# Pass 1 of a hybrid decoder layer: the work behind each turning transfer issued after k's and q's; triangles turned in pass 1, q and k kept by 512 tokens

## The chip, the cores and the metric

One core of a Trainium2 chip runs the whole program. The metric is the device time of one execution in microseconds (us), the median of three runs. A smaller time is better.

## What is computed

One decoder layer over 2048 tokens of width 1024, all in float32 to the outside. In the reference, cut to what matters:

```python
a = _rmsnorm(h, g_in[i])                                   # 2048 x 1024
z = einsum('bsd,de->bse', a, w_in[i])                      # 1024 -> 4*512 + 3*512
q, k, v, gate_b, u_a, v_a, gate_a = split(z)
q = _rope(_rmsnorm(q, q_norm[i]), positions)               # 8 heads of 64
k = _rope(_rmsnorm(k, k_norm[i]), positions)
o_b = _dilated_attention(q, k, v) * silu(gate_b)           # (window, dilation): (128,1),(512,4),(2048,16)
o_a = _gmlp_spatial(u_a, v_a, w_spatial[i], b_spatial[i], ln_v_g[i], ln_v_b[i]) * silu(gate_a)
h = h + einsum('bse,ed->bsd', concatenate([o_b, o_a]), w_out[i])
gate = sigmoid(_rmsnorm(h, g_ple[i]) @ w_ple_gate[i] + b_ple_gate[i])
h = h + gate * (p[i] @ w_ple_proj[i])
```

`_gmlp_spatial` multiplies each chunk of 128 tokens by four lower triangles of 128x128 (`w_spatial`), which must be turned (transposed) once. The three branches of the attention are merged with weights from their softmax denominators.

## The kernel before, in words

**Pass 1** (0 to 388 us) goes over 16 tiles of 128 tokens. `prep(n)` makes the normed and turned tile: sum of squares on ACT (L210), scale on DVE (L147, L216) with a power on POOL (L148), a copy of the 16-bit halves of each word to two staging tiles on ACT (L179), two transposing DMAs on SP's queue (L181), a copy back on DVE (L183), and a split of each half into a high part on ACT (L193) and a low part on DVE (L194). The result is the tile `aT`. It then stores the turned tile (L499) and loads the x of a later tile (L233). `turn_p` does the same with the tile p of the per-layer input, without the split.

`step(n, g)` multiplies `aT` of tile n with the weights of one of q, k, v and the gate g of the attention, 24 matmuls of 128x512 each (L227), in the PSUM banks `mm`, `s`, `av` and `gt`. After k's and q's product `post_qk` squares on ACT (L405), reduces on DVE (L407), rotates with two products on DVE (L413, L415) and a sum on POOL (L114), takes a power on POOL (L148), scales on DVE (L420), and splits the result into a high half `hl` on ACT (L422) and a low half on DVE (L423). `turn_qk` turns `hl` with one transposing DMA into `st` (L429); for k an ACT copy regroups `st` (L432); then it is stored to d_q or d_k (L435). `post_v` scales and stores v (L442, L443), `post_gb` takes a tanh on ACT (L451) and a multiply on DVE (L452), which free the gate's bank.

Within pass 1 a scheduler sets the order of every engine's instructions from the data they need and its own estimate of when each is ready. The code's order is only its start. Every engine works through its list in that order: an instruction that waits holds up what stands behind it on the same engine. `issue_after(i)` allows nothing that is issued inside it to be placed before instruction i. PE's order is written by hand from the last two tiles of pass 1 on.

**Pass 2** (388 to about 860 us) is the attention, four pairs of heads with 38 steps each (scores L755, exponentials, turning of the weights by DMA L777, values L791). Into it PE's order mixes the three gMLP products u, v_A and gate_A as filler (L627): first `BLOCK0` us of them ahead of the first scores, then `FILL` us per step. Their weights come in 24 pieces of 256 KB through four staging tiles called `raw` (L127, copied by L133 on ACT and DVE and L135 on POOL). q and k come from d_q and d_k in chunks (`load_qk`), the chunks of the next pair during the steps of the current one. **Pass 3** (860 to 1293 us) is the output projection and the per-layer embedding.

Buffers that matter here: `stage()` hands out the `raw` tiles in turn; `aT` has two buffers in one pool and one in another; the x of tile n+2 is loaded into the buffer that tile n leaves.

Of the kernel before, what the change touches and what calls it, by code (L numbers as in the profile page):

```python
# [10 lines left out]
F32 = mybir.dt.float32  # L11
# [43 lines left out]
BLOCK0, FILL = 18, 1.3  # L55
# [9 lines left out]
STAGE = {"g": "m1 m2 vt hl st", "q": "m1 m2 vt hl st", "k": "vt", "v": ""}  # L65
# [16 lines left out]
def hybrid_layer(ctx: ExitStack, tc: tile.TileContext, io, out):  # L82
# [11 lines left out]
    d_qk = [dram.tile([128, HEADS, S], F16, name=f"d_{n}") for n in "qk"]  # L94
# [10 lines left out]
    cst.tile([128, 16], F32, name="pad")  # L105
# [66 lines left out]
    def turn_words(src, turned):  # L172
# [24 lines left out]
    def turn_rows(src, dst, turned):  # L197
        turn_words(src, turned)
        split_words(turned, dst)
# [6 lines left out]
    def norm_T(xt, xn, pool, turned=None, gain=None):  # L206
# [10 lines left out]
        if turned is None:  # L217
            split_T(xn, 8, aT, whole=gain is not None)
        else:
            turn_rows(xn, aT, turned)  # L220
# [48 lines left out]
    with ExitStack() as s1, ExitStack() as s1q:  # L269
# [6 lines left out]
        ORDER = "gqkv"  # L276
# [114 lines left out]
        TAB = {}  # L391
# [10 lines left out]
        def post_qk(n, which, ps):  # L402
# [19 lines left out]
            nc.scalar.activation(hl[:, :, 0], r, AF.Copy)  # L422
            nc.vector.tensor_tensor(hl[:, :, 1], r, hl[:, :, 0], op=OP.subtract)  # L423
            return hl

        def turn_qk(n, which, hl):
# [8 lines left out]
            nc.sync.dma_start(d_qk[which][:, :, n * 128:(n + 1) * 128], st)  # L435
# [13 lines left out]
        def post_gb(n, ps):  # L449
            g = p1g.tile([128, 512], F32, name="gb")  # L450
# [6 lines left out]
        def gm_constants():  # L457
            for name, src in (("lng", bcast(io["ln_v_g"], 512)), ("lnb", bcast(io["ln_v_b"], 512)),
                              ("mask", io["c_mask"]), ("bs", io["b_spatial"][0].rearrange("g t -> t g")),
                              ("gg", io["w_spatial"][0].rearrange("g t s -> t g s"))):  # L460
                shape = {"mask": [128, 512], "bs": [128, 4]}.get(name, [128, 512])
                CG[name] = pg.tile(shape, F32, name=name)
                dst = CG[name]
                nc.sync.dma_start(dst if name != "gg" else dst.rearrange("p (g s) -> p g s", g=4), src)

        def spatial_weights():

            wsT, gg, bs = pg.tile([128, 4, 128], F32, name="wsT"), CG["gg"], CG["bs"]
            CG["wsT"] = wsT
            keep = stage()[:, 0:128]  # L470
            nc.vector.tensor_scalar(keep, CG["mask"][:, 384:512], 0.0, None, op0=OP.is_ge)
            pt = bank("pt", (128, 4, 128))
            for g in range(4):
                w = gg[:, g * 128:(g + 1) * 128]
                last = nc.vector.scalar_tensor_tensor(w, w, 0.25, keep, op0=OP.mult, op1=OP.mult)
                nc.tensor.transpose(pt[:, g], w, ident)
            nc.vector.tensor_copy(wsT, pt)
            with tc.issue_after(last.ins):
                nc.vector.tensor_scalar(bs, bs, 0.25, None, op0=OP.mult)
# [11 lines left out]
        def prep(n):  # L491
            if n < NT:
                xt = XT.pop(n)
# [463 lines left out]
```

## Time and profile before

| | |
|---|---|
| Median of three runs | 1290.81 us (1289.02, 1290.81, 1296.98) |
| Profiled execution | 1295.01 us, span 1293.2 us |
| PE busy | 1201.3 us, 93% of the span |
| DVE, ACT, POOL busy | 888.2 (69%), 648.9 (50%), 512.1 us (40%) |
| Mean granted clock of TensorE | 0.976 |
| PE by stage | 0 to 40 us start; 160 to 340 us 168.41 of 180 busy; 388 to 442 us 33.24 of 54 busy; 860 to 1293 us 420.87 of 433 busy |

A granted clock of 1.00 is TensorE at 2.4 GHz, 0.50 at 1.2 GHz. PE is the engine to watch: on it each gap has an engine or a DMA that ended last, and the profile names it in brackets behind the row.

### The profile page before, as it was taken

The numbers are of one execution on the slowest core, as the hardware profiler recorded it, in microseconds if no ns is written. First come the engines' busy times: TensorE is split into PE (matmuls) and PEld (weight loads), VectorE is DVE, ScalarE is ACT, GpSimd is POOL, SyncE is SP. The second block draws the span as 40 slices with busy tenths as digits, with TensorE's granted clock in tenths as the row PEclk, the third lists the DMA queues.
The fourth block names the chain that finished last, engine by engine and source line by source line (L and its number), as shares of the span: only waits on it lengthen the run. The fifth ranks groups of instructions, "written<-read, shape, count | busy, mean of one in ns | idle before, by whom it ended". The sixth has DMA issues, their size and how long they took to land.

```text
span 1293.2 us, 21329 instructions
## 1 busy us (share of the span) xinstructions
PE 1201.3 (93%) x7166; PEld 976.0 (75%) x7166; DVE 888.2 (69%) x2253; ACT 648.9 (50%) x1273; POOL 512.1 (40%) x454
## 2 busy tenths in 40 slices
PE   5999999989995799899799799879999999999998
PEld 4778877767884687687687688768778888888887
DVE  5885565655575678778778678598766766666733
ACT  5754334334344577677677677444334434434422
POOL 4852343433453456555555565342212121221100
PEclk9999999999997899899999999989999999999999
DMA  7598777776769899999999999955555655654531
GB/s 263 160 229 197 168 183 166 165 180 157 175 171 239 202 202 220 219 216 236 218 217 223 219 229 215 207 176 174 141 147 123 165 156 128 153 162 127 143 90 49
DMA packets 442254, 233.21 MB, mean 180 GB/s; under 512 B 337440, under 2 KB 392864, under 8 KB 442144
## 3 DMA queue, kind: packets, MB, share of 16 engines
q1 hardware_dynamic: 442144, 231.85, 75.4%
q8 instruction: 56, 0.92, 0.3%
q14 instruction: 54, 0.44, 0.1%
HBM read 102.66 MB, written 57.28 MB: 124 GB/s over the span
## 4 chain that ended last, share of the span: by engine, by line
PE 41%; DMA 19%; DVE 16%; ACT 7%; issue 7%; POOL 6%; SPq 4%; DVEq 0%; ACTq 0%; POOLq 0%
PE mm L227 17%; PE mm L627 8%; PE gt L227 5%; DMA pt<-raw 4%; DMA xt<-raw 3%; PE s L227 3%; DMA st<-hl 3%; PE s L755 3%; PE pt L791 2%; DVE aT L194 2%; DMA ob<-d_o 2%; ACT raw L179 2%; POOL rsh L148 2%; DVE m L420 1%; DVE pr L758 1%
## 5 line engine op out<-in xcount | busy, mean ns | idle before, releaser
L227 PE MATMUL mm<-wslot,aT 128*128 128x512 f32 x1536 | 362.8, 392 | 7.8 <-ACT aT L193 3.3
L227 PEld LDWEIGHTS mm<-wslot,aT 128*128 128x128 f32 x1536 | 289.4, 189 | 70.4 <-ACT aT L193 4.6
L627 PE MATMUL mm<-wslot,aT 128*128 128x512 f32 x1152 | 317.9, 418 | 23.2 <-DVE raw L618 14.2
L627 PEld LDWEIGHTS mm<-wslot,aT 128*128 128x128 f32 x1152 | 214.1, 197 | 63.5 <-DVE raw L618 14.6
L114 POOL TENSOR_TENSOR raw<-pr,raw 128x512 f16<-128x512 f32 (+1 forms) x152 | 178.0, 1177 | 151.6 <-ACT raw L773 137.9
L766 ACT ACTIVATE pr<-pr,ost 128x256 f32<-128x256 f32 (+1 forms) x384 | 150.5, 451 | 78.8 <-DVE ost L764 70.9
L227 PE MATMUL gt<-wslot,aT 128*128 128x512 f32 x744 | 177.8, 393 | 6.1 <-DVE gb L452 5.3
L227 PEld LDWEIGHTS gt<-wslot,aT 128*128 128x128 f32 x744 | 139.8, 189 | 38.0 <-DVE gb L452 7.0
L791 PEld LDWEIGHTS <-pt 128*128 128x128 f16 x1800 | 66.3, 99 | 62.1 <-issue 33.7
L773 ACT ACTIVATE raw<-pr 128x512 f16<-128x512 f32 (+1 forms) x152 | 93.2, 620 | 39.6 <-DMA pt<-raw 37.4
L791 PE MATMUL pt<-sv,pt 128*128 128x65 f16 x1800 | 83.6, 196 | 21.8 <-DMA pt<-raw 21.8
L758 DVE CUSTOM_DVE_ANT_0 pr<-s,mask 128x256 f32<-128x256 f32 (+1 forms) x256 | 81.3, 359 | 29.7 <-POOL raw L114 16.0
L227 PE MATMUL av<-wslot,aT 128*128 128x512 f32 x360 | 86.0, 392 | 7.3 <-DVE gb L452 6.3
L227 PE MATMUL s<-wslot,aT 128*128 128x512 f32 x384 | 90.0, 390 | 1.6 <-POOL wslot L135 1.6
L114 POOL TENSOR_TENSOR m<-m,m 128x512 f32<-128x512 f32 x32 | 47.9, 1498 | 94.8 <-DVE rsh L147 88.8
L227 PEld LDWEIGHTS av<-wslot,aT 128*128 128x128 f32 x360 | 67.2, 188 | 23.6 <-DVE gb L452 7.9
L227 PEld LDWEIGHTS s<-wslot,aT 128*128 128x128 f32 x384 | 72.0, 188 | 17.0 <-POOL wslot L135 2.0
L755 PEld LDWEIGHTS <-sq 128*128 128x128 f16 x768 | 70.4, 121 | 13.7 <-issue 7.4
L755 PE MATMUL s<-sk,sq 128*128 128x256 f16 (+1 forms) x512 | 73.7, 279 | 7.0 <-DMA sk<-d_k 6.1
L566 POOL TENSOR_TENSOR ma<-ob,ma 128x512 f32<-128x512 f32 x16 | 24.5, 1533 | 122.1 <-DMA ma<-d_gb 58.0
L563 POOL TENSOR_TENSOR ob<-ob 128x512 f32<-128x512 f32 x16 | 21.0, 1314 | 126.5 <-DVE ob L561 126.5
L764 DVE TENSOR_SCALAR ost<-ost 128x2 f32<-128x2 f32 (+1 forms) x152 | 66.9, 442 | 2.6
(209 smaller groups left out, 1723.4 us busy)
## 6 DMA issues: line engine op xcount, KB each, us to landing
xt<-x SPq DMA_DIRECT2D x32, 512.0 KB, 4.6
d_o<-ost SPq DMA_DIRECT2D x48, 264.0 KB, 3.2
raw<-w_in SPq DMA_DIRECT2D x38, 256.0 KB, 3.7
sv<-d_vt SPq DMA_DIRECT2D x32, 264.0 KB, 3.5
ob<-d_o SPq DMA_DIRECT2D x16, 528.0 KB, 4.6
xt<-d_at SPq DMA_DIRECT2D x16, 512.0 KB, 5.0
out<-th SPq DMA_DIRECT2D x32, 256.0 KB, 2.8
d_at<-raw SPq DMA_DIRECT2D x28, 256.0 KB, 2.5
```

Of the source, the lines that this page charges most:

```text
L114: nc.gpsimd.tensor_tensor(dst, a, b, op=op)
L148: nc.gpsimd.tensor_tensor(dst, dst, mhalf[:, :width], op=OP.pow)
L179: nc.scalar.activation(turned[t].bitcast(U16), words[:, t], AF.Copy)
L194: nc.vector.tensor_tensor(lo, f, hi.bitcast(F32), op=OP.subtract)
L227: nc.tensor.matmul(ps, aT[:, ha, k, :], w(slot, hw, k), start=(n == 0), stop=(n == 3 * nk - 1))
L627: nc.tensor.matmul(ps, GT[c][:, ha, k, :], slots[g][:, hw, k, :], start=(n == 0), stop=(n == 23))
L755: nc.tensor.matmul(ps[:, c:c + nk], cols(br, j, Q[h]), cols(br, j, K, n, h, self.nb), start=(n == 0), stop=(n == 1))
L758: nc.vector.tensor_tensor_reduce(pr[:, c:c + nk], ps[:, c:c + nk], mask[:, m - nk:m], -1.0, 3e38, op0=OP.add, op1=OP.min, accum_out=o[:, j ...
L764: nc.vector.tensor_scalar(nm, nm, math.log(PSCALE), None, op0=OP.add)
L766: nc.scalar.activation(pr[:, c:c + nk], pr[:, c:c + nk], AF.Exp, bias=o[:, j - j0, 130 + h:131 + h], scale=-1.0)
L773: nc.scalar.activation(ph, pr[:, :width], AF.Copy)
L791: nc.tensor.matmul(PO[0][:, j % 2, h], self.pt[:, t, c // 128], vt[:, h, vv, 0:65], start=(n == 0), stop=(n == 3 * self.nb - 1))
```

## The change

It has five parts. (1) In pass 1 k's product comes ahead of q's, and what follows a turning transfer of x or p (copy back, split, stores, load of the next x) is collected in `rest` and issued by `finish` behind the last two instructions of q's `post_qk` of the tile before. (2) The triangles are turned at tile 3 of pass 1 and kept in DRAM (`d_ws`) until pass 2 loads them. (3) d_q and d_k are laid out by 512 tokens; a chunk is two loads of q (128 KB) and two of k (256 KB), where it was two of q and four of k; the last two chunks of a pair come apart and not as one. A narrow step (256 wide) is turned by one DMA, where it was two. (4) The gates of the last two tiles go to `raw` tiles; the first gMLP chunk uses its pool's tile and not a `raw` tile. (5) `BLOCK0` goes from 18 to 11.

```diff
-BLOCK0, FILL = 18, 1.3
+BLOCK0, FILL = 11, 1.3
...
-STAGE = {"g": "m1 m2 vt hl st", "q": "m1 m2 vt hl st", "k": "vt", "v": ""}
+STAGE = {"g": "m1 m2 vt hl st", "k": "m1 m2 vt hl st", "q": "vt", "v": ""}
...
-    d_qk = [dram.tile([128, HEADS, S], F16, name=f"d_{n}") for n in "qk"]
...
+    d_qk = [dram.tile([128, 4, HEADS, 512], F16, name=f"d_{n}") for n in "qk"]
+    d_ws = dram.tile([128, 512], F32, name="d_ws")
...
-        for i in range(2):
-            nc.vector.tensor_copy(turned[i].bitcast(U16).rearrange("p (k c t) -> p t k c", t=2, k=nk),
-                                  halves[:, :, i * nk:i * nk + nk])
+        def back():
+            for i in range(2):
+                nc.vector.tensor_copy(turned[i].bitcast(U16).rearrange("p (k c t) -> p t k c", t=2, k=nk),
+                                      halves[:, :, i * nk:i * nk + nk])
+        if rest is None:
+            back()
+        else:
+            rest.append(back)
...
-    def turn_rows(src, dst, turned):
-        turn_words(src, turned)
-        split_words(turned, dst)
+    def turn_rows(src, dst, turned, rest=None):
+        turn_words(src, turned, rest)
+        if rest is None:
+            split_words(turned, dst)
+        else:
+            rest.append(lambda: split_words(turned, dst))
...
-    def norm_T(xt, xn, pool, turned=None, gain=None):
+    def norm_T(xt, xn, pool, turned=None, gain=None, rest=None):
...
     AT, GT, XT, slots = {}, {}, {0: xt0}, {}
     usc = cst.tile([128, 1], F32, name="usc")
-    def load_qk(qk, hp, c, n=1):
-        tl = slice(512 * c, 512 * (c + n))
+    def load_qk(qk, hp, c):
+        hs = slice(2 * hp, 2 * hp + 2)
         for h in range(2):
-            nc.sync.dma_start(qk[0][h][:, tl], d_qk[0][:, 2 * hp + h, tl])
-            yield
+            nc.sync.dma_start(qk[0][h][:, 512 * c:512 * c + 512], d_qk[0][:, c, 2 * hp + h])
+        yield
+        src = d_qk[1][0:64, c, hs]
         for i in (0, 64):
-            for t in range(2):
-                nc.sync.dma_start(qk[1][i:i + 64, t, :, tl], d_qk[1][64 * t:64 * t + 64, 2 * hp:2 * hp + 2, tl])
-            yield
+            nc.sync.dma_start(qk[1][i:i + 64, c].rearrange("p t h s -> p t (h s)"),
+                              bass.AP(tensor=src.tensor, offset=src.offset,
+                                      ap=[[4 * HEADS * 512, 64], [64 * 4 * HEADS * 512, 2], [1, 1024]]))
+        yield
     gating, s2 = ExitStack(), ExitStack()
     with ExitStack() as s1, ExitStack() as s1q:
...
-        ORDER = "gqkv"
+        ORDER = "gkqv"
...
             r = m1.rearrange("p h t d -> p h (t d)")
             nc.vector.tensor_tensor(r, r, rs[:, :, None].to_broadcast([128, HEADS, 64]), op=OP.mult)
             hl = p1.tile([128, HEADS, 2, 64], F16, name="hl", bufs=2)
-            nc.scalar.activation(hl[:, :, 0], r, AF.Copy)
-            nc.vector.tensor_tensor(hl[:, :, 1], r, hl[:, :, 0], op=OP.subtract)
+            LAST[:] = [nc.scalar.activation(hl[:, :, 0], r, AF.Copy).ins,
+                       nc.vector.tensor_tensor(hl[:, :, 1], r, hl[:, :, 0], op=OP.subtract).ins]
             return hl
         def turn_qk(n, which, hl):
...
-            nc.sync.dma_start(d_qk[which][:, :, n * 128:(n + 1) * 128], st)
+            nc.sync.dma_start(d_qk[which][:, n // 4, :, n % 4 * 128:n % 4 * 128 + 128], st)
...
-            g = p1g.tile([128, 512], F32, name="gb")
+            g = p1g.tile([128, 512], F32, name="gb") if n < NT - 2 else stage()
...
 def spatial_weights():
+            gg, keep = stage(), stage()
+            nc.sync.dma_start(gg.rearrange("p (g s) -> p g s", g=4),
+                              io["w_spatial"][0].rearrange("g t s -> t g s"))
+            nc.sync.dma_start(keep[:, 0:128], io["c_mask"][:, 384:512])
+            nc.sync.dma_start(bs, io["b_spatial"][0].rearrange("g t -> t g"))
+            nc.vector.tensor_scalar(keep[:, 0:128], keep[:, 0:128], 0.0, None, op0=OP.is_ge)
+            ps = bank("pt", (128, 4, 128))
+                nc.vector.scalar_tensor_tensor(w, w, 0.25, keep[:, 0:128], op0=OP.mult, op1=OP.mult)
+                nc.tensor.transpose(ps[:, g], w, ident)
+            nc.vector.tensor_copy(gg, ps.rearrange("p g s -> p (g s)"))
+            nc.sync.dma_start(d_ws, gg)
+            nc.vector.tensor_scalar(bs, bs, 0.25, None, op0=OP.mult)
...
             else:
                 (post_v if g == "v" else post_gb)(n, ps)
-        def prep(n):
-            if n < NT:
-                xt = XT.pop(n)
-                turned = None if n < PE1 else (stage(), stage())
-                AT[n] = norm_T(xt, xt, p1g if n % 3 == 2 else stream, turned, gbc)
+        def prep(n, rest=None):
+            xt = XT.pop(n)
+            turned = None if n < PE1 else (stage(), stage())
+            AT[n] = norm_T(xt, xt, p1g if n % 3 == 2 else stream, turned, gbc, rest)
+            def store():
                 if turned is None:
                     nc.sync.dma_start(d_at[n], xt)
                 for i, t in enumerate(turned or ()):
                     nc.sync.dma_start(d_at[n][:, 512 * i:512 * i + 512], t)
-                tables(n)
                 if n + 2 < NT:
                     XT[n + 2] = load_x(x_t[n + 2])
-        def turn_p(n):
+            tables(n)
+            if rest is None:
+                store()
+            else:
+                rest.append(store)
+        def turn_p(n, rest):
             t = stage()
             pp, turned = two(t)
             nc.sync.dma_start(pp, io["p"][0, 0][n * 128:(n + 1) * 128])
-            turn_words(pp, two(turned))
-            nc.sync.dma_start(d_p[n], turned)
+            turn_words(pp, two(turned), rest)
+            rest.append(lambda: nc.sync.dma_start(d_p[n], turned))
+        def finish(rest):
+            with tc.issue_after(LAST[0]), tc.issue_after(LAST[1]):
+                for f in rest:
+                    f()
         prep(0)
         prep(1)
...
                 v_scale()
             for n in range(2):
                 step(n, g)
-        for n in range(2, NT - 2):
-            prep(n)
-            for m in range(max(0, n - 4) * NT // 10, max(0, n - 3) * NT // 10):
-                turn_p(m)
-            if n > 2:
-                for g in "qkvg":
+        for n in range(2, NT):
+            rest = []
+            prep(n, rest)
+            if n == 3:
+                spatial_weights()
+            for m in range(max(0, n - 4) * NT // 10, min(NT, max(0, n - 3) * NT // 10)):
+                turn_p(m, rest)
+            if n == 2:
+                for f in rest:
+                    f()
+                continue
+            if n < NT - 1:
+                for g in "kq":
                     step(n - 1, g)
-        for g in "qkvg":
-            step(NT - 3, g)
-        prep(NT - 2)
-        prep(NT - 1)
+            finish(rest)
+            if n < NT - 1:
+                for g in "vg":
+                    step(n - 1, g)
         in_order = ExitStack()
         in_order.enter_context(tc.manual_schedule(engines={mybir.EngineType.PE}))
         XT[0] = load_x(d_at[0])
         gm_rows(0, stream)
-        for g in "qkv":
+        for g in "kqv":
             for n in (NT - 2, NT - 1):
                 step(n, g)
         s1q.close()
...
-            t = pool.tile([128, 512], F32, name=name, bufs=n) if c else stage()
+            t = pool.tile([128, 512], F32, name=name, bufs=n)
...
-                self.pt = pt = p2.tile([128, 2, 4, 128], F16, name="pt", bufs=PH)
-                if width == 512:
-                    nc.sync.dma_start_transpose(pt.rearrange("p t k q -> p (t k) q"),
-                                                hl.rearrange("p t c -> p (t c)"))
-                else:
-                    for t in range(2):
-                        nc.sync.dma_start_transpose(pt[:, t, :width // 128], hl[:, t, :width])
+                pt = p2.tile([128, 8, 128], F16, name="pt", bufs=PH)[:, 0:width // 64]
+                nc.sync.dma_start_transpose(pt, hl.rearrange("p t c -> p (t c)"))
+                self.pt = pt.rearrange("p (t k) q -> p t k q", t=2)
...
-                        h, c = {10: (1, 0), 11: (1, 1), 0: (0, 2)}.get(i % 12, (4, 0))
-                        loads = load_qk(qk, hp + h, c, 1 + c // 2) if i > 1 and hp + h < 4 else iter(())
+                        h, c = {10: (1, 0), 11: (1, 1), 0: (0, 2), 1: (0, 3)}.get(i % 12, (4, 0))
+                        loads = load_qk(qk, hp + h, c) if i > 1 and hp + h < 4 else iter(())
```

Names: `LAST` is filled by `post_qk`; `two(t)` gives the halves of a staging tile; `rows_T` gives an `aT`; the lines of the changed kernel are some 10 to 33 higher than before.

**ACT, one tile in the middle of pass 1.** Before (`gb` is the gate's tanh, `aT,ss<-xt` the sum of squares, `hl<-st` the regrouping of the turned k, `raw<-xt` the copy of x's words, `raw<-raw` that of p's, `sq` the squares of q's or k's product, `hl<-m` the high half; `mm` holds q's product and `s` k's):

```order
L451 ACTIVATE gb<-gt 128x512
L210 ACTIVATE aT,ss<-xt 128x1024
L432 ACTIVATE hl<-st 128x1024
L179 ACTIVATE raw<-xt 128x1024 x2
L405 ACTIVATE sq<-mm 128x512
L179 ACTIVATE raw<-raw 128x256 x2
L193 ACTIVATE aT<-raw 128x512
L405 ACTIVATE sq<-s 128x512
L193 ACTIVATE aT<-raw 128x512
L422 ACTIVATE hl<-m_2118 128x8x64
L442 ACTIVATE vt<-gt,sv 128x8x64
L422 ACTIVATE hl<-m_2163 128x8x64
```

and in the changed kernel, from k's high half of one tile to q's squares of the next:

```order
L436 ACTIVATE hl<-m_1155 128x8x64
L456 ACTIVATE vt<-av,sv 128x8x64
L446 ACTIVATE hl<-st 128x1024
L436 ACTIVATE hl<-m_1201 128x8x64
L465 ACTIVATE gb<-gt 128x512
L202 ACTIVATE aT<-raw 128x512 x2
L183 ACTIVATE raw<-xt 128x1024 x2
L222 ACTIVATE aT,ss<-xt 128x1024
L183 ACTIVATE raw<-xt 128x1024
L419 ACTIVATE sq<-s 128x512
L183 ACTIVATE raw<-raw 128x256 x2
L419 ACTIVATE sq<-mm 128x512
```

The two splits to `aT` stood among the squares of q's and k's; they now stand behind q's high half and the gate's tanh, ahead of k's squares of the tile that they are for. k's regrouping moved ahead of q's high half.

On PE the 96 matmuls of a tile came as 24 of q, 24 of k, then v and the gate. Now come 4 of k, 4 of q and 4 of the gate, then the rest of k and of q, so that k's last is the 33rd and q's last the 52nd, then 24 of v and the other 20 of the gate.

**DVE, the same place in the changed kernel** (`L188` copies back, first x's and then p's; `L203` is the low part of `aT`, `L466` frees the gate's bank):

```order
L434 TENSOR_TENSOR m_961<-m_961,rsh 128x512
L437 TENSOR_TENSOR hl<-m_961,hl 128x8x64
L457 SCALAR_TENSOR_TENSOR vt<-gt,sv,vt 128x8x64
L434 TENSOR_TENSOR m_1007<-m_1007,rsh 128x512
L437 TENSOR_TENSOR hl<-m_1007,hl 128x8x64
L188 COPY raw<-xt 128x2x512 x2
L188 COPY raw<-raw 128x2x128 x2
L466 SCALAR_TENSOR_TENSOR gb<-gb,av 128x512
L203 TENSOR_TENSOR aT<-raw,aT 128x512 x2
L150 TENSOR_SCALAR rs<-ss 128x1
```

The copies back stand behind q's low half (`hl<-m_1007,hl`); before, they stood between the rotation of q and that of k.

**SP's queue at the end of pass 1.** Before (`w_in` is the weights' pieces, `st<-hl` the turning of q or k):

```order
L127 DMA raw<-w_in 128x512 x4
L429 DMA_TRANSPOSE st<-hl 128x8x128
L127 DMA raw<-w_in 128x512 x2
L435 DMA d_q<-st 1024x1x128
L127 DMA raw<-w_in 128x512 x2
L429 DMA_TRANSPOSE st<-hl 128x8x128
L127 DMA raw<-w_in 128x512
L435 DMA d_q<-st 1024x1x128
L127 DMA raw<-w_in 128x512 x2
```

and in the changed kernel:

```order
L475 DMA mask<-c_mask 128x512
L475 DMA wsT<-d_ws 128x512
L475 DMA lng<-ln_v_g 128x512
L475 DMA lnb<-ln_v_b 128x512
L467 DMA d_gb<-raw 128x512
L273 DMA sq_3472<-d_q 128x512
L130 DMA raw<-w_in 128x512 x2
L467 DMA d_gb<-raw 128x512
L130 DMA raw<-w_in 128x512
L273 DMA sq_3473<-d_q 128x512
```

The pieces stood among q's and k's last transfers; all 24 now stand behind the last stores of pass 1 and the first load of q, whose tile `sq` takes room that pass 1 held until its last matmul.

**SP's queue towards the second pair of heads.** Before:

```order
L265 DMA sk<-d_k 64x2x512 x2
L777 DMA_TRANSPOSE pt<-raw 128x8x128
L672 DMA d_oa<-gg 128x512
L265 DMA sk<-d_k 64x2x512 x2
L777 DMA_TRANSPOSE pt<-raw 128x8x128
L261 DMA sq_3454<-d_q 128x1024
L729 DMA sv<-d_vp 128x4x264
L777 DMA_TRANSPOSE pt<-raw 128x8x128
L261 DMA sq_3455<-d_q 128x1024
L781 DMA_TRANSPOSE pt<-raw 128x2x128 x2
L800 DMA d_o<-ost 128x528
L265 DMA sk<-d_k 64x2x1024 x2
```

and in the changed kernel:

```order
L277 DMA sk<-d_k 64x2x1024
L809 DMA_TRANSPOSE pt<-raw 128x8x128
L277 DMA sk<-d_k 64x2x1024
L273 DMA sq_3472<-d_q 128x512
L809 DMA_TRANSPOSE pt<-raw 128x8x128 x2
L762 DMA sv<-d_vp 128x4x264
L829 DMA d_o<-ost 128x528
L809 DMA_TRANSPOSE pt<-raw 128x8x128
L809 DMA_TRANSPOSE pt<-raw 128x4x128
L809 DMA_TRANSPOSE pt<-raw 128x8x128 x2
L273 DMA sq_3473<-d_q 128x512
L277 DMA sk<-d_k 64x2x1024 x2
```

Four loads of k for a chunk became two of twice the width, and the narrow turning (`L781`, two of 128x2x128) became one (128x4x128).

## Rows read from the trace of the kernel before

**Rows 1.** PE by stretch: us, busy (instructions), granted clock, DMA share, GB/s.

```profile
160.00:340.00 180.00, 168.41 (x733) 1.00 0.72 170
340.00:388.00 48.00, 48.00 (x213) 1.00 0.73 177
...
860.00:1293.00 433.00, 420.87 (x1848) 0.99 0.50 136
```

**Rows 2.** PE's timeline in pass 1: start, us, operation [idle before <-releaser].

```profile
268.57 5.60 PE L227 MATMUL gt<-wslot,aT 128*128 128x512 f32 x24
274.01 5.60 PE L227 MATMUL mm<-wslot,aT 128*128 128x512 f32 x24
...
287.29 5.74 PE L227 MATMUL gt<-wslot,aT 128*128 128x512 f32 x24 [2.24 <-DVE gb L452]
```

**Rows 3.** DVE's timeline in pass 1.

```profile
269.60 0.69 DVE L407 TENSOR_REDUCE ssh<-sq 128x8 f32<-128x512 f32 x1 [3.82 <-ACT sq L405]
...
270.80 0.74 DVE L415 TENSOR_TENSOR m<-mm,tb 128x256 f32<-128x256 f32 x2
271.46 0.16 DVE L147 TENSOR_SCALAR rsh<-ssh 128x8 f32<-128x8 f32 x1
...
273.90 1.40 DVE L183 COPY raw<-xt 128x1024 uint16<-128x1024 uint16 x2 [2.28 <-DMA xt<-raw]
...
277.62 0.68 DVE L420 TENSOR_TENSOR m<-m,rsh 128x512 f32<-128x512 f32 x1
...
279.48 1.27 DVE L147 TENSOR_SCALAR rsh<-ssh 128x8 f32<-128x8 f32 x1
...
284.56 0.68 DVE L420 TENSOR_TENSOR m<-m,rsh 128x512 f32<-128x512 f32 x1
285.94 0.69 DVE L423 TENSOR_TENSOR hl<-m,hl 128x512 f16<-128x512 f32 x1 [0.69 <-ACT hl L422]
```

**Rows 4.** ACT's timeline in pass 1.

```profile
268.99 0.58 ACT L405 ACTIVATE sq<-mm 128x512 f32<-128x512 f32 x1
...
274.75 0.64 ACT L193 ACTIVATE aT<-raw 128x512 fp32r<-128x512 f32 x1 [2.40 <-DVE raw L183]
...
285.82 0.58 ACT L451 ACTIVATE gb<-gt 128x512 f32<-128x512 f32 x1
...
290.63 1.11 ACT L432 ACTIVATE hl<-st 128x1024 f16<-128x1024 f16 x1 [3.20 <-DMA st<-hl]
```

**Rows 5.** POOL's timeline in pass 1.

```profile
277.78 0.84 POOL L396 TENSOR_TENSOR ta<-gA,cs 128x128 f32<-128x128 f32 x1 [3.09 <-DVE m L413]
279.11 1.60 POOL L114 TENSOR_TENSOR m<-m,m 128x512 f32<-128x512 f32 x1 [0.49 <-DVE m L415]
```

**Rows 6.** PE's timeline in pass 2, a longer wait.

```profile
504.05 0.54 PE L791 MATMUL pt<-sv,pt 128*128 128x65 f16 x12 [2.40 <-DMA pt<-raw]
...
504.79 2.75 PE L627 MATMUL mm<-wslot,aT 128*128 128x512 f32 x6
```

**Rows 7.** PE by stretch, behind that wait (columns as in rows 1).

```profile
506.00:508.00 2.00, 2.00 (x16) 0.50 1.16 295
```

**Rows 8.** PE's timeline from pass 1 into pass 2.

```profile
387.87 11.04 PE L627 MATMUL mm<-wslot,aT 128*128 128x512 f32 x48
413.10 7.19 PE L627 MATMUL mm<-wslot,aT 128*128 128x512 f32 x24 [14.19 <-DVE raw L618]
...
442.14 0.61 PE L791 MATMUL pt<-sv,pt 128*128 128x65 f16 x6 [5.84 <-DMA pt<-raw]
```

**Rows 9.** SP's queue, pieces of the weights: start, us, operation.

```profile
373.68 1.36 SPq L127 DMA_DIRECT2D raw<-w_in  x2
...
402.90 0.71 SPq L127 DMA_DIRECT2D raw<-w_in  x1
```

**Rows 10.** DMA issues on the page: operation xcount, KB each, us to landing.

```profile
xt<-x SPq DMA_DIRECT2D x32, 512.0 KB, 4.6
...
raw<-w_in SPq DMA_DIRECT2D x38, 256.0 KB, 3.7
```

**Rows 11.** PE's waits in pass 2: us in total, times, longest.

```profile
PE pt L791 <- DMA pt<-raw: 21.8, 14, 5.8
PE s L755 <- DMA sk<-d_k: 6.1, 6, 1.9
```

More of the change, by code (lines that the diff above doesn't have):

```diff
@@ L102, in hybrid_layer @@
     d_o = dram.tile([12, S, OW], F32, name="d_o")
-    cst.tile([128, 16], F32, name="pad")
+    cst.tile([128, 8], F32, name="pad")
+    bs = cst.tile([128, 4], F32, name="bs")
     ident = cst.tile([128, 128], F32, name="ident")
@@ L170, in two, with turn_words @@
         return t[:, 0:n], t[:, n:2 * n]
-    def turn_words(src, turned):
+    def turn_words(src, turned, rest=None):
         words = src.bitcast(U16).rearrange("p (c t) -> p t c", t=2)
@@ L219, in norm_T @@
         else:
-            turn_rows(xn, aT, turned)
+            turn_rows(xn, aT, turned, rest)
         return aT
@@ L389, in v_scale @@
             nc.vector.tensor_copy(usc, e_i[:, 1:2].bitcast(F32))
-        TAB = {}
+        TAB, LAST = {}, []
         def tables(n):
@@ L457, in gm_constants @@
         def gm_constants():
[L458 to L464, printed above, removed]
@@ L466, in spatial_weights @@
-        def spatial_weights():
[L468 to L472, printed above, removed]
+            for name, src in (("mask", io["c_mask"]), ("wsT", d_ws),
+                              ("lng", bcast(io["ln_v_g"], 512)), ("lnb", bcast(io["ln_v_b"], 512))):
+                CG[name] = pg.tile([128, 512], F32, name=name)
+                nc.sync.dma_start(CG[name], src)
@@ L473, in spatial_weights @@
             for g in range(4):
                 w = gg[:, g * 128:(g + 1) * 128]
[L475 to L479, printed above, removed]
+                nc.vector.scalar_tensor_tensor(w, w, 0.25, keep[:, 0:128], op0=OP.mult, op1=OP.mult)
@@ L660, in gm_g @@
             pool_tt(t, t, G["u", c], OP.mult)
-            if c == 0:
-                spatial_weights()
-            wsT, bs = CG["wsT"], CG["bs"]
+            wsT = CG["wsT"].rearrange("p (g s) -> p g s", g=4)
             pq = bank("gt" if c < NT - TAIL else "s", (128, 4, 128))
@@ L697, in cols, with at @@
                 return t[:, t0:t0 + 127 * st + 1:st]
+            def at(c):
+                return c // 512 * 2048 + c % 512
             if br == 0:
-                start, back, dims = 128 * j, 128, [[1, 128]]
+                start, back, dims = at(128 * j), at(128 * (j - 1)), [[1, 128]]
             elif br == 1:
-                start, back, dims = j // 4 * 512 + 32 * (j % 4), 512, [[128, 4], [1, 32]]
+                start, dims = j // 4 * 2048 + 32 * (j % 4), [[128, 4], [1, 32]]
+                back = start - 2048
             else:
-                start, back, dims = 32 * (j % 4) + j // 4, 0, [[128, 16], [4, 8]]
+                start, dims = 32 * (j % 4) + j // 4, [[2048, 4], [128, 4], [4, 8]]
             if blocks == 2:
-                start, dims = start - back, [[back, 2]] + dims
-            a = t[:, part, h]
+                start, dims = back, [[start - back, 2]] + dims
+            a = t[:, 0, part, h]
             return bass.AP(tensor=a.tensor, offset=a.offset + start, ap=[list(a.ap[0])] + dims)
@@ L816, in hybrid_layer @@
         qk = ([p2.tile([128, S], F16, name="sq" + n) for n in "01"],
-              p2.tile([128, 2, 2, S], F16, name="sk"))
+              p2.tile([128, 4, 2, 2, 512], F16, name="sk"))
         loads = iter(())
```

4 lines of the change are left out of this document (2 added, 2 removed).

## The prediction, made before the changed kernel ran

> **What bounds the kernel now.** I read PE's busy time by stretch first, then PE's own waits, then the lists of the engines that end those waits. PE is full in the last stretches of pass 1 and nearly so in pass 3; between 160 and 340 us it stands still for 180 − 168.41 = 11.6 us [rows 1]. So pass 3, which the change leaves alone, stays as it is, and pass 1 has at most 11.6 us to give back here. Eight waits make up these 11.6 us, all before the third product of a tile, on the DVE instruction that frees the gate's bank; the longest is 2.24 us [rows 2]. A product of 24 matmuls takes 274.01 − 268.57 = 5.44 us [rows 2], so a tile needs 4 × 5.44 = 21.76 us of PE. Otherwise PE stands still where pass 1 ends (14.19 and 5.84 us [rows 8]) and in pass 2 on turned weights and on k [rows 11].
>
> **Pass 1, the main term.** Before, the split of a tile's `aT` ran a whole product or more ahead of the product that used it: ACT split at 274.75 [rows 4], and this tile's first product began at 298.30. In the changed kernel ACT's list has the split behind the gate's tanh of the tile before, and that waits for the gate's last matmul. So PE must wait after each gate for tanh and split, 0.58 + 0.64 us [rows 4] with about 0.15 us of handing over: 1.37 us, at 12 tiles (3 to 14) 16.4 us. That is the floor, 16.4 − 11.6 = **+4.8 us** against the waits that it replaces, because k is no longer fed ahead of time. The old wait for the gate's bank goes: the bank is now freed at the start of a tile and next wanted by v some 12 us later.
>
> A second chain ends at the same split, and I take it to be the longer. It starts at q's 52nd matmul, 52/24 × 5.44 = 11.79 us after the tile's start, and runs through
> - q's squares 0.58 [rows 4], reduction 0.69, rotation 0.68 and 0.74 [rows 3] and the small scale, 0.16 us at 271.46 [rows 3] (1.27 us at 279.48 with POOL in the way, which I keep for the upper end);
> - k's scaling 0.68, then ACT's high half 0.64 (the split's row, same size) and DVE's low half 0.69 [rows 3, 4];
> - k's turning transfer: low half done at 285.94 + 0.69 = 286.63, ACT's regrouping at 290.63, so 4.0 us, then the regrouping's 1.11 us [rows 3, 4];
> - only now, since ACT has the regrouping ahead of it, q's high half 0.64 and low half 0.69;
> - and, since `finish` ties it to those two, the copy back 0.70 (half of 1.40 [rows 3]) and the split 0.64.
>
> The sum is 24.4 us from the tile's start; DVE's rows overlap by about 0.08 us each and handovers cost about 0.05 us, so 24.2 us. PE idles 24.2 − 21.76 = 2.4 us in each of 12 tiles: 29 − 11.6 = **+17 us**. DVE's copies back of p, its work for the gate and the low parts come after that, under PE's first 12 matmuls of the new tile (2.7 us), which need only high parts; I cost them at nothing, and at most 0.5 us per tile if that cover is too short.
>
> The load of x for the next tile but one also moves behind the split: it lands 4.6 us after its issue [rows 10], two stores later. Tiles mostly use it late, but at four of them ACT has a copy of its words (row `raw<-xt` ahead of `sq<-s`) that waits for it and stands ahead of k's squares. I count 1.5 us each (nothing if k's squares are still in time, 2.4 us if not): **+6 us**.
>
> A wait of 2.24 us in pass 1 left the granted clock of the stretch at 1.00 [rows 1, 2]; one of 2.40 us in pass 2 was followed by 0.50 [rows 6, 7], that is 1.2 GHz and not 2.4. There six matmuls took 2.75 us [rows 6], which is twice 6/24 of 5.44 us, so 1.4 us were lost on them; with the smaller ones beside them I take 1.6 us per fall. I count it for the four longer waits: **+6 us**. For 2.4 us I leave it out and keep it as a rival.
>
> The triangles' few operations on DVE and four turnings on PE now lie beside the products of tile 3: **+1 us** (0 if covered, 3 if k's chain has to wait for all of them).
>
> **From pass 1 to pass 2.** Before, 18 pieces of weights went out between 373.68 and 402.90 us, 1.72 us apart [rows 9], in part under the last products, so PE could run 48 matmuls from 387.87 on; then it waited 14.19 us; the first values began at 442.14, 54.3 us after the last matmul of pass 1, with 118 filler matmuls done [rows 8]. In the changed kernel none of the 24 pieces goes out before pass 1's last matmul. At 1.72 us that is 39.6 us, with landing (3.7 us [rows 10]) and copy 44 us; four staging tiles that turn over in 3.7 us and a copy of at most 1.6 us (POOL's pass over as many elements [rows 5]) would do it in 23 × 1.33 + 5 = 35 us. ACT and DVE have less beside it than before, so I take 40. Scores and filler run meanwhile; the exponentials stand on ACT behind the last piece, and splits and turning of one step are 0.64 + 0.69 + 4.0 = 5.3 us in pass 1's rows [rows 3, 4]; with the exponentials and the lag of the next step I take twice that, 11 us: first values some 51 us after pass 1, with 84 filler matmuls done. That wins 3 us, and 34 matmuls of 5.44/24 us (7.7 us) are still to run: **+4.4 us** (−3 to +10). The waits of 14.19 and 5.84 us are thus not gained; waiting for the weights takes their place.
>
> **Pass 2.** Per chunk two loads of k leave SP's queue, and per pair of heads one narrow turning. The waits on k, 6.1 us in all [rows 11], mostly go; of the 21.8 us on turned weights [rows 11] those near a new pair of heads, where SP's queue is full, shrink, and the clock falls behind them too. I take **−12 us**: k's 6, a fifth of the others' 22 and one fall of the clock. The ends are −4 (SP's queue stays full, only some of k's waits go) and −22 (k's, half of the others' and three falls).
>
> **The sum:** +17 + 6 + 6 + 1 + 4.4 − 12 = +22 us on the profiled execution of 1295.0 us: 1317. That execution stands 4.2 us above the median of the runs, so by the runs' median 1313.
>
> **Rivals.**
> - *The clock falls at nearly every tile of pass 1.* For it: 2.4 us is just the wait that brought a fall in pass 2; against it: 2.24 us brought none here. Eight more falls of 1.6 us and waits of up to 3 us, if DVE's small scale takes 1.27 us again: +13 + 7, so 1333.
> - *Faster: the floor decides.* If the chain behind q is shorter than 23.1 us, a microsecond less than I add up, say because k's turning lands sooner, the tanh and split alone are left: +4.8 in pass 1, no late x, no fall, −3 at the boundary, and −17 in pass 2. The sum is −15: 1276 by the median. For it: several durations in the chain are taken from rows in which the engine was also waiting for others. Against it: each link of the chain has a row, and the scheduler's list puts it in this order on both engines.
> - *It cancels.* A chain between the two (23.5 us), two late loads, one fall, and −15 in pass 2: 12 × 1.75 − 11.6 + 3 + 2 + 1 + 2 − 15 = +2: 1293.
> - *DVE stands still beside POOL.* The trace shows that the small scale on DVE takes 1.27 us while POOL sums, and ends with it [rows 3, 5]; but a scaling of 512 elements took 0.68 us with POOL's table product beside it (277.78) as with POOL idle (284.56) [rows 3, 5]. If it did wait for POOL, k's scaling would, in the new order, stand behind POOL's sum for q, 1.60 us, in 12 tiles: +19 us, so 1332. The Trainium skill ("SBUF — State Buffer", Who interferes with whom) has the rule for this: a DVE instruction with two inputs in SBUF blocks fully against a POOL instruction that reads SBUF. By that rule 1332 would be right; the two rows of 0.68 us speak against it here.
> - *The change doesn't do what it says*: the lists show that it does, so only its effect is open.
>
> **Chances.** The forecast (1300 to 1325) 0.45; falling clock 0.17; DVE beside POOL 0.04; a boundary with more than 10 us lost 0.04; cancelling 0.17; floor, faster 0.13. About 1%, 13 us, is what a measurement of this kernel can tell from no change: faster than 1278 is about 0.13, within 1% (the cancelling case and the forecast's lower end) 0.23, slower than 1304 then 0.64. The range of 8 in 10 reaches from 1282, which leaves out most of the faster case, to 1336, past the falling clock. The likeliest case's own range is 1300 to 1325.
>
> **What would show it.** In the changed profile, PE's wait before each tile's first product (`s`, k's) on ACT's `aT` split, 12 times, 1.4 us by the floor and about 2.4 us by the chain; the period from one k to the next 23.1 or 24.2 us; ACT's list with q's high half right behind the regrouping. The old waits on the gate's bank gone. The granted clock in 160 to 340 us below 1.00 if the falls come. The pieces of the weights starting only at the end of pass 1 and PE idle there for more than 14 us. In pass 2 fewer than 2 us of waits on k. The forecast is wrong if PE's waits in pass 1 are under 12 us in all, or if the end of pass 1 hardly moves.

## The result and the profile after

The changed kernel takes 1336.95 us (median of four runs, 1333.55 to 1340.07) where the kernel before took 1291.99 us beside it: 1.0343 times as long, 95% interval 1.030 to 1.0387. The direction was as forecast; the size was twice the forecast, and just past the range's upper end.

The page of the changed kernel:

```profile
span 1331.8 us, 21290 instructions
...
PE 1216.3 (91%) x7166; PEld 980.7 (74%) x7166; DVE 868.2 (65%) x2253; ACT 655.1 (49%) x1273; POOL 516.8 (39%) x454
```

PE's busy time grew by 15 us against the page before, with as many matmuls (7166 records in both) and a mean granted clock of 0.969 where it was 0.976: that is time at the lower clock. The rest of the longer span is waiting.

One division into three stages serves for all kernels here. It goes by the end of pass 1 (the end of PE's last matmul `pt<-wslot,aT`), the start of the first values (`pt<-sv,pt`), and the end. The filler matmuls done in the middle stage differ in number, so each one missing of 118 is added there at 5.44/24 = 0.227 us and taken off the rest. All in us, from each kernel's timeline of PE and its span:

| kernel | pass 1 ends | to first values, with 118 filler matmuls | the rest | span |
|---|---|---|---|---|
| before | 388.0 | 54.1 | 851.1 | 1293.2 |
| changed | 422.9 | 66.1 | 842.8 | 1331.8 |
| nothing deferred (e1) | 393.3 | 70.7 | 839.6 | 1303.6 |
| last gates in own buffer (e2) | 421.9 | 42.1 | 838.9 | 1302.8 |
| layout alone (e3) | 383.5 | 51.1 | 841.5 | 1276.1 |
| tied to k (e4) | 377.8 | 65.9 | 846.4 | 1290.1 |
| e1 and e2 | 395.2 | 48.7 | 842.9 | 1286.8 |
| e4 and e2 | 379.0 | 40.7 | 844.0 | 1263.7 |
| e4, e2, BLOCK0 18 | 379.9 | 37.5 | 842.4 | 1259.8 |
| k regrouped on POOL (e9) | 423.6 | 66.3 | 843.8 | 1333.7 |

The change thus cost 34.9 us in pass 1 and 12.0 us behind it, and gave back 8.3 us later: +38.6 us between the two profiled executions. By the medians it is +45 us, since the profiled execution of before lay above its median and that of the change was the fastest of its four.

**Pass 1.** PE's waits between 100 and 420 us (us in total, times, longest), which answer to [rows 1, 2]:

```profile
PE s L239 <- ACT aT L202: 28.7, 11, 3.6
```

The waits on the gate's bank are gone, and this one stands in their place. Six rows of PE's timeline show four of the waits and what followed two of them:

```profile
123.92 1.20 PE L239 MATMUL s<-wslot,aT 128*128 128x512 f32 x4 [2.30 <-ACT aT L202]
124.95 1.74 PE L239 MATMUL mm<-wslot,aT 128*128 128x512 f32 x4
...
200.66 1.20 PE L239 MATMUL s<-wslot,aT 128*128 128x512 f32 x4 [1.88 <-ACT aT L202]
...
225.16 1.20 PE L239 MATMUL s<-wslot,aT 128*128 128x512 f32 x4 [2.45 <-ACT aT L202]
226.19 1.07 PE L239 MATMUL mm<-wslot,aT 128*128 128x512 f32 x4
...
277.08 1.20 PE L239 MATMUL s<-wslot,aT 128*128 128x512 f32 x4 [3.36 <-ACT aT L202]
```

Behind the wait of 2.30 us four matmuls of q took 1.74 us, behind that of 2.45 us the same four took 1.07. The chain that ends at 225.16, on ACT:

```profile
213.29 0.58 ACT L419 ACTIVATE sq<-mm 128x512 f32<-128x512 f32 x1
...
221.43 1.12 ACT L446 ACTIVATE hl<-st 128x1024 f16<-128x1024 f16 x1 [2.53 <-DMA st<-hl]
222.45 0.61 ACT L436 ACTIVATE hl<-m 128x512 f16<-128x512 f32 x1
...
224.47 1.26 ACT L202 ACTIVATE aT<-raw 128x512 fp32r<-128x512 f32 x2 [0.93 <-DVE raw L188]
```

and on DVE:

```profile
217.21 1.00 DVE L437 TENSOR_TENSOR hl<-m,hl 128x512 f16<-128x512 f32 x1 [0.70 <-ACT hl L436]
...
220.17 0.69 DVE L434 TENSOR_TENSOR m<-m,rsh 128x512 f32<-128x512 f32 x1 [0.49 <-POOL rsh L151]
223.10 0.69 DVE L437 TENSOR_TENSOR hl<-m,hl 128x512 f16<-128x512 f32 x1 [2.24 <-ACT hl L436]
223.71 1.35 DVE L188 COPY raw<-xt 128x1024 uint16<-128x1024 uint16 x2
```

q's squares at 213.29, k's high and low half to 218.21, the turning of k, its regrouping from 221.43, q's high half behind it, q's low half at 223.10, copy back, the first split done about 225.1, and PE starts: each step follows on the one before. The tile took 225.16 − 200.66 = 24.5 us, where the prediction added up 24.2. That the sum fits so well is in part luck: k's low half took 1.00 us and not 0.69 and q's squares began 0.6 us late, behind ACT's copy of p's words, but k's turning took 3.2 us (218.21 to 221.43) and not 4.0.

**The granted clock** behind two of these waits (columns as in [rows 1]):

```profile
124.00:128.00 4.00, 4.00 (x12) 0.64 1.03 266
...
277.10:281.10 4.00, 4.00 (x18) 1.00 1.06 251
```

**The end of pass 1** on PE, answering to [rows 8], and on SP's queue, answering to [rows 9]:

```profile
411.83 11.04 PE L239 MATMUL pt<-wslot,aT 128*128 128x512 f32 x48
429.00 1.43 PE L659 MATMUL mm<-wslot,aT 128*128 128x512 f32 x2 [6.14 <-ACT wslot L136]
...
442.35 6.74 PE L659 MATMUL mm<-wslot,aT 128*128 128x512 f32 x20 [2.30 <-ACT wslot L136]
...
466.29 0.40 PE L788 MATMUL av<-sk,sq 128*128 128x128 f16 x4
```

```profile
421.19 0.43 SPq L467 DMA_DIRECT2D d_gb<-raw  x1
422.90 0.33 SPq L273 DMA_DIRECT2D sq<-d_q  x1
423.27 0.96 SPq L130 DMA_DIRECT2D raw<-w_in  x2
424.33 0.38 SPq L467 DMA_DIRECT2D d_gb<-raw  x1
426.41 0.33 SPq L130 DMA_DIRECT2D raw<-w_in  x1
```

PE stands still for 6.14 us and then in short pieces for each piece of weights; the first scores come at 466.29. SP begins with the weights at 423.27, and the third piece stands behind the store of the last gate at 424.33.

**Pass 2**, PE's waits on turned weights from the first values on, before (442.5 to 860 us) and after (460 to 900 us), answering to [rows 11]:

```profile
PE pt L791 <- DMA pt<-raw: 15.9, 13, 3.2
```

```profile
PE pt L820 <- DMA pt<-raw: 23.5, 19, 4.3
```

No wait on k is left in the changed kernel. The waits on turned weights grew: of the 21.8 us in [rows 11], 5.84 us are the wait ahead of the first values, which the table counts in the middle stage. So PE stands still as long as it did. The rest, from the first values to the end, before and after (columns as in [rows 1]):

```profile
442.14:1293.20 851.06, 808.62 (x5454) 0.98 0.76 175
```

```profile
481.29:1331.80 850.51, 809.25 (x5489) 0.99 0.76 176
```

PE was idle for 42.4 us before and for 41.3 us after. Its busy time holds 34 filler matmuls more after (7.7 us) and is still only 0.6 us longer. Of the 8.3 us that were gained, some 7 are thus PE at a higher granted clock, and 1 is waiting.

### The profile page after: what moved, and what is told of

The parts are those of the page before. It is cut to its first block, busy times and chain, and to the rows that moved or that the text cites. A ratio compares the mean times of both kernels' runs of the same rounds, so it can differ in the third digit from the quotient of the medians.

```text
span 1331.8 us, 21290 instructions
## 1 busy us (share of the span) xinstructions
PE 1216.3 (91%) x7166; PEld 980.7 (74%) x7166; DVE 868.2 (65%) x2253; ACT 655.1 (49%) x1273; POOL 516.8 (39%) x454
## 4 chain that ended last, share of the span: by engine, by line
PE 52%; DMA 18%; DVE 9%; ACT 4%; issue 4%; POOL 4%; SPq 2%; DVEq 0%; POOLq 0%; ACTq 0%
PE mm L239 20%; PE mm L659 9%; PE gt L239 7%; PE s L239 7%; DMA pt<-raw 6%; PE s L788 3%; DMA raw<-w_in 3%; PE pt L820 2%; DMA st<-hl 2%; PE av L239 2%; DMA ob<-d_o 1%; DMA d_vp<-vt 1%; PE av L788 1%; DVE pr L791 1%; DVE aT L203 1%
## 5 line engine op out<-in xcount | busy, mean ns | idle before, releaser
L239 PE MATMUL mm<-wslot,aT 128*128 128x512 f32 x1536 | 367.8, 393 | 1.7 <-ACT aT L202 1.4
L659 PE MATMUL mm<-wslot,aT 128*128 128x512 f32 x1152 | 323.2, 420 | 30.2 <-ACT wslot L136 23.3
L239 PE MATMUL gt<-wslot,aT 128*128 128x512 f32 x744 | 181.1, 396 | 1.0 <-ACT wslot L136 1.0
L239 PE MATMUL s<-wslot,aT 128*128 128x512 f32 x384 | 100.5, 408 | 37.7 <-ACT aT L202 34.6
L239 PE MATMUL av<-wslot,aT 128*128 128x512 f32 x360 | 88.7, 395 | 2.4 <-ACT wslot L136 2.3
L151 POOL TENSOR_TENSOR rs<-rs,mhalf 128x1 f32<-128x1 f32 x32 | 20.3, 633 | 160.8 <-DVE rs L150 158.2
```

The source lines that it names most:

```text
L151: nc.gpsimd.tensor_tensor(dst, dst, mhalf[:, :width], op=OP.pow)
L239: nc.tensor.matmul(ps, aT[:, ha, k, :], w(slot, hw, k), start=(n == 0), stop=(n == 3 * nk - 1))
L659: nc.tensor.matmul(ps, GT[c][:, ha, k, :], slots[g][:, hw, k, :], start=(n == 0), stop=(n == 23))
```

## The experiments

Theory A, formed from these rows: pass 1 loses because the split of `aT` is tied to the end of q's chain; the stretch behind it loses because the last two gates hold staging tiles that the weights need; the layout gives some 8 to 12 us. Rivals: k's product ahead of q's or too few staging tiles cost pass 1 its time (B); the load of q or the shorter filler block holds up the weights (C); the layout only renames waits (D).

**e1: nothing deferred.**

```diff
-            finish(rest)
+            for f in rest:          # right behind prep(n) and turn_p(m)
+                f()
```

> The changed kernel, except that what follows a turning transfer is issued at once, ahead of k's and q's work, and not behind q's last two instructions. Theory A (PE waits for each tile's aT because its split stands behind q's chain): PE's waits before k's product fall from 34.6 us to under 15 us, the granted clock in pass 1 is back at 1.00, pass 1 is 25 to 33 us shorter; time 1304 to 1312. Rival B (the loss in pass 1 comes from k's product ahead of q's, or from too few staging tiles, whatever the place of the split): the waits stay above 25 us, time 1325 to 1337.

Measured: 1306.63 us, 1.0100 of before (1.0079 to 1.0122). PE's waits from 60 to 430 us:

```profile
PE mm L658 <- ACT wslot L136: 24.0, 6, 11.8
PE gt L239 <- DVE gb L466: 5.8, 4, 2.6
PE av L239 <- DVE gb L466: 3.6, 3, 2.1
PE s L239 <- ACT aT L202: 1.7, 1, 1.7
```

The wait on the split is down to one of 1.7 us and the old wait on the gate's bank is back. Theory A holds for these waits and B falls: k's product is still first, the staging tiles are as few. Pass 1 is still 5.3 us longer than before; tile 2 begins at 72.63 us and not at 68.14, and which part of the change delays this start no run shows. The wait for weights stays.

**e2: the last gates in their own buffer.**

```diff
-            g = p1g.tile([128, 512], F32, name="gb") if n < NT - 2 else stage()
+            g = p1g.tile([128, 512], F32, name="gb")
```

> The changed kernel, except that the gates of the last two tiles go to their own buffer as before and not to staging tiles. Theory A (the staging tiles that the gates hold keep the 24 pieces of weights behind the end of pass 1): the pieces start before pass 1's last matmul, PE's waits on weights (27 us) go down to some 15, pass 1 itself stays as long as in the changed kernel; time 1322 to 1330. Rival C (the pieces are late because the first load of q waits for pass 1's last matmul, or because of the shorter filler block): no change, 1333 to 1340.

Measured: 1305.67 us, 1.0092 (1.0072 to 1.0113): 31 us less than the changed kernel where 7 to 15 were expected. PE's rows, and the first and the last pieces of weights that SP issued between 395 and 445 us:

```profile
410.82 11.04 PE L239 MATMUL pt<-wslot,aT 128*128 128x512 f32 x48
421.70 11.04 PE L659 MATMUL mm<-wslot,aT 128*128 128x512 f32 x48
...
442.22 0.59 PE L788 MATMUL av<-sk,sq 128*128 128x128 f16 x4 [7.36 <-DMA sk<-d_k]
```

```profile
397.02 1.92 SPq L130 DMA_DIRECT2D raw<-w_in  x3
...
424.55 0.90 SPq L130 DMA_DIRECT2D raw<-w_in  x2
```

Pieces go out before the end of pass 1 again, 48 filler matmuls run without a gap, and the stretch to the first values is 42.1 us and not 66.1. The first load of q still comes behind pass 1's end (436.46) and `BLOCK0` is still 11, so rival C falls. The cause is as theory A has it, its size was underestimated: what was counted as the boundary's loss against before (12 us) hid a gain of 12 us against before, which appears once the weights are in time. The wait of 14.19 us [rows 8] is not there. It ended on the activation of the first gMLP chunk in a `raw` tile (L618), which part (4) moves to another tile; no run takes this alone, nor the triangles turned earlier. What ends the wait before the first scores now is k's load (7.36 us).

**e3: the layout alone, on the kernel before** (d_q, d_k, `load_qk`, `sk` and the narrow turning as in the change).

> The kernel before, with the third part alone: q and k laid out and loaded by 512 tokens, narrow steps turned by one transfer. Theory A: the waits on k in pass 2 (7.5 us) go and those on turned weights shrink a little: 7 to 12 us shorter, 1280 to 1286. Rival D (SP's queue stays as full, so the waits only change their name): 1289 to 1294.

Measured: 1278.13 us, 0.9877 (0.9861 to 0.9894), some 15 us less than before and 2 us better than expected. Waits from 440 to 840 us:

```profile
PE pt L792 <- DMA pt<-raw: 18.9, 26, 2.4
```

The waits on k are gone; those on turned weights are 18.9 us where they were 15.9, in 26 shorter pieces. The rest after the first values is 9.6 us shorter: 3.5 us less idle and 6.0 us less busy time of PE for the same matmuls. So rival D is right about part of it, and more than half of the gain is the granted clock. Another 4.5 us lie in pass 1, whose code here differs only in where k and q are stored: its waits on the gate's bank came to 6.4 us where they were 11.6, and why is not shown.

**e4: tied to k's last two instructions and not to q's.**

```diff
-                for g in "kq":
-                    step(n - 1, g)
+                step(n - 1, "k")
+                kept = list(LAST)
+                step(n - 1, "q")
+                LAST[:] = kept
```

> The changed kernel, with what follows a turning transfer tied to k's last two instructions and not to q's. Theory A (the chain through k's turning transfer, its regrouping and q's high half sets the wait): that chain is out of it, the split comes some 6 us earlier and ahead of the gate's tanh; PE's waits before k's product fall from 34.6 us to under 12, time 1302 to 1312. Rival B: above 25 us of waits, 1325 to 1337.

Measured: 1288.10 us, 0.9953 (0.9932 to 0.9974), 49 us less than the changed kernel and below every bound that was given. PE between 100 and 370 us (us, busy, clock, DMA share, GB/s):

```profile
100.00:370.00 270.00, 270.00 (x1193) 1.00 0.77 185
```

PE does not stand still once, and the clock stays at 1.00: neither the old wait nor the new one is there. ACT's list now has the split behind k's high half, ahead of v and of the gate's tanh. In pass 1 the deferral itself helps by 15 us (e4's 377.8 against e1's 393.3); tying it to q is what cost.

**e9: the regrouping of k on POOL**, with the deferral as in the change:

```diff
-                nc.scalar.activation(sp..., st..., AF.Copy)
+                nc.gpsimd.tensor_copy(sp..., st...)
```

> The changed kernel, except that k's regrouping after its turning transfer is done on POOL and not on ACT; what follows a turning transfer stays tied to q. Theory A (on ACT q's high half, and with it the split, waits behind k's turning transfer): q's high half and the split come 4 to 5 us sooner; PE's waits before k's product fall from 34.6 to under 8 us, pass 1 ends at 380 to 388 us, time 1295 to 1304. Rival G (the gate's tanh ahead of the split, or SP's queue, sets the wait): the waits stay at 16 us or more, time 1312 to 1337.

Measured: 1330.99 us, 1.0288 (1.0259 to 1.0317). Theory A's expectation was wrong, by its own number:

```profile
PE s L239 <- ACT aT L202: 31.6, 12, 4.8
```

DVE and POOL in one tile:

```profile
221.86 0.69 DVE L434 TENSOR_TENSOR m<-m,rsh 128x512 f32<-128x512 f32 x1 [1.29 <-POOL rsh L151]
223.24 1.56 DVE L437 TENSOR_TENSOR hl<-m,hl 128x512 f16<-128x512 f32 x1 [0.70 <-ACT hl L436]
```

```profile
220.18 1.64 POOL L151 TENSOR_TENSOR rsh<-rsh,mhalf 128x8 f32<-128x8 f32 x1
223.18 1.08 POOL L446 COPY hl<-st 128x1024 f16<-128x1024 f16 x1 [1.35 <-DMA st<-hl]
```

With the regrouping out of ACT's list q's high half waits for q's own scaling, which waits for POOL's power of q (220.18 + 1.64 = 221.82). Over the eleven tiles that begin between 98 and 354 us the high half came 21.7 us after the tile's start, where it came 22.7 us after it in the changed kernel: 1.0 us sooner, and not 4 to 5. The split behind it came no sooner (24.6 and 24.7 us), and POOL's copy beside DVE's work takes up most of that: in the tile shown the low half took 1.56 us and not 0.69.

In this tile, which began at 199.32, the high half even came 1.5 us later (23.3 us after the start, against 21.8 in the tile from 200.66 above). The edit also moved the start of the chain. ACT has the sum of squares of the next x ahead of k's squares, and waits there for the load of x; ACT's waits from 100 to 380 us, in the changed kernel and in e9:

```profile
ACT aT L222 <- DMA xt<-x: 19.8, 11, 7.0
```

```profile
ACT aT L222 <- DMA xt<-x: 47.3, 11, 5.7
```

k's squares thus began 11.2 us after the start of this tile and not 8.3. Time and waits are where rival G had them. The gate's tanh is not the reason, as it stands behind the first half of the split in all eleven tiles; whether SP's queue is, through the load of x, no run separates. So e9 does not show which link of q's chain sets the wait. What is shown is that the tie to q does (e1, e4): e4 leaves every link of q's behind.

**e5: nothing deferred and the last gates in their own buffer** (the edits of e1 and e2).

> The changed kernel with nothing deferred and the last gates in their own buffer: layout, triangles, k ahead of q and the shorter filler block are left. Theory A: pass 1 ends at 393 us as with nothing deferred, 881 us from there: 1272 to 1280, so no better than the layout alone. Rival E: 1285 to 1300.

Measured: 1288.25 us, 0.9959 (0.9945 to 0.9974): a miss by 8 us. Waits from 60 to 440 us:

```profile
PE mm L659 <- DVE gv L650: 9.0, 1, 9.0
PE gt L240 <- DVE gb L467: 5.6, 4, 2.4
PE av L240 <- DVE gb L467: 5.3, 5, 2.3
PE av L788 <- DMA sk<-d_k: 4.7, 1, 4.7
```

Pass 1 is as expected (395.2). The stretch behind it is 48.7 us and not 42.1, with waits for `gv` (9.0 us) and for k. The second repair is worth about as much here (70.7 − 48.7 = 22.0 us) as on the changed kernel (24.0) and beside e4 (25.2). What theory A missed is that e1 had made this stretch 4.6 us longer (70.7 against 66.1), and the rest is 4 us longer than in e2. The time lies within rival E's range; its reason is not shown.

**e6 and e8: both repairs, and then `BLOCK0` back at 18.** The edits are those of e4 and e2, and for the second `BLOCK0, FILL = 18, 1.3`.

> The changed kernel with both repairs: what follows a turning transfer tied to k's last two instructions, and the last gates in their own buffer. Theory A (the two costs lie one behind the other and don't share anything): pass 1 ends at 378 us as with the first repair, and from there it takes 881 us as with the second: 1256 to 1264. Rival E (part of the one cost hides the other, the weights then compete with the end of pass 1): 1268 to 1280.

> As the changed kernel with both repairs, and the filler block ahead of the first scores back at 18 us. In the run with the gates in their own buffer PE waited 7.4 us for k before the first scores. Theory A: the longer block covers that wait, 4 to 8 us less than with both repairs alone: 1250 to 1257. Rival F (filler run early is missing later): the same time within 2 us.

Measured: 1261.86 us, 0.9753 (0.9737 to 0.9769), and 1256.64 us, 0.9721 (0.9701 to 0.9742). Both as theory A expected. Waits of the second from 60 to 440 us:

```profile
PE pt L822 <- DMA pt<-raw: 4.4, 1, 4.4
PE s L239 <- ACT aT L202: 2.0, 1, 2.0
```

The longer filler block (88 matmuls ahead of the first scores, where both repairs alone have 52) fills the wait for k, which was 5.4 us with both repairs alone. This version beats the kernel before by 36 us and the changed one by 80.

## Why the prediction was right in its kind and wrong in its size

- **Pass 1** (forecast +30 in all, measured +34.9). The place and the chain were right: the wait is before k's product, on the split, in 12 tiles, and its steps follow one another as added up. Eleven waits make 28.7 us, and the twelfth, at tile 3 (98.09 us), was 3.98 us: 32.7 − 11.6 = 21 us against 23. The late x came in four tiles, as forecast: there ACT's copy of its words stands ahead of k's squares, and the waits that follow are 3.57, 2.81, 2.93 and 3.60 us. The other eight are 2.5 us on average, where 2.4 was forecast, so by these averages the late x cost 0.8 us each and not 1.5. Every wait is above the floor of 1.37 us. The clock fell behind six of the twelve (2.30, 2.81, 2.93, 3.57, 3.60 and 3.98 us, but not 3.36), four were counted; a fall cost about the 1.6 us assumed (q's product ended 13.7 us after the tile's start where it ended 12.1 without). And 3.4 us came before tile 2, which began at 71.55 us and not at 68.14; I had taken the start for unchanged.
- **The end of pass 1** (forecast +4.4, range −3 to +10, measured +12.0). This is the step that failed: "In the changed kernel none of the 24 pieces goes out before pass 1's last matmul ... I take 40". The lateness was right, the reason given with the change (the load of q and the room of `sq`) was not enough: the load of q did stand ahead of the pieces on SP's queue (422.90), but e2, which leaves it as it is, shows that the two gates in staging tiles put the pieces there. The last piece was copied at 469.7, so 47 us after pass 1 and not 40: the 44 us that I had from [rows 9] was the nearer end. The first values came 58.4 us after pass 1 where 51 was forecast, with the 84 filler matmuls that were forecast. PE's waits in this stretch came to 23.4 us against 20.9 before; the rest of the 12.0 us is PE's time at a lower granted clock (0.71 against 0.86), for which I had no term. Whether a higher clock alone would have shortened the stretch no run shows, as the weights set its end. And with the cause wrong I never asked what part (4) costs: it reads like housekeeping, and its gates alone were worth 31 us (e2).
- **Pass 2** (forecast −12, measured −8.3). The waits on k went, as forecast. The waits on turned weights grew by about 8 us, where I took a fifth of them off. What made up for it is PE's granted clock, some 7 us, for which I had counted one fall (1.6 us). So the size is near the forecast by luck; its terms are not.
- **The rivals.** The falling clock (1333 us) came nearest in time, though only six of its twelve falls came; the time is rather the sum of three terms that each erred to the same side (5 + 8 + 4 us), with 6 us between the profiled executions and the medians on top. The faster rival needed a chain shorter than 23.1 us; e4 shows that this end was within reach of the same deferral by one small edit. *DVE beside POOL* (1332 us) was near in time too, but its 19 us did not come: in the tile shown k's scaling (215.83, 0.68 us) began ahead of POOL's sum (215.99) and did not wait. Still I read my rows too fast there, and the last section says how.
- **The range.** It took each term's likely value, and its upper end held one rival only; the upper ends that the text names (per tile 1.1 us for the small scale and 0.5 us for the cover, +10 at the boundary, −4 in pass 2), taken together, would have reached past 1340.

## What to carry to other kernels

Where work is tied to "behind X", add up the chain that ends in X and compare it with the period: in this kernel q's chain ended after the next product was due, k's did not, and one small edit between them was worth 49 us. A shared staging pool is a queue: two tiles lent to something that lived until the end of a stage held up every prefetch through that pool, at 31 us. When one chain is taken away and nothing moves, look for a second that ends close behind it, and for what the edit itself moved, and measure both from the tile's start. When waits go and the time follows, check whether waiting or the clock changed.

## What the runs showed of the hardware that was not expected

The clock did not follow the length of the wait: 3.36 us left it at 1.00 and 2.30 us brought 0.64 over the next 4 us; e4, with no wait, kept 1.00 through 270 us. What decides is not shown here.

DVE and POOL do hold each other up, and in these rows the one that began second waits. In the changed kernel POOL's rows read

```profile
211.57 1.29 POOL L117 TENSOR_TENSOR m<-m,m 128x512 f32<-128x512 f32 x1 [3.46 <-DVE rsh L150]
...
215.26 0.47 POOL L410 TENSOR_TENSOR ta<-gA,cs 128x128 f32<-128x128 f32 x1 [0.79 <-DVE m L427]
215.99 1.68 POOL L117 TENSOR_TENSOR m<-m,m 128x512 f32<-128x512 f32 x1 [0.26 <-DVE rsh L150]
```

The table product took 0.47 us here and 0.84 us in [rows 5], where DVE's scaling had begun first: there POOL waited, and DVE's scaling showed no delay [rows 3]. The sum took 1.29 us alone and 1.68 us begun at 215.99 just after DVE's scaling; DVE's low half, begun at 217.21 under that sum, took 1.00 us and not 0.69, and 1.56 us beside POOL's copy in e9. This is what the Trainium skill states ("SBUF — State Buffer", Who interferes with whom: the one that issues first holds the port, the other blocks); these rows agree with it, though the low halves end some 0.15 us before a full wait for POOL would let them, and against what the prediction took from two of them. At 0.3 to 0.9 us per instruction it was a small part of a tile's 24 to 27 us.
